# Forgetting attention on one core: second exponentials in place, normalizing one step later, VectorE's work in written order

## The chip, the cores and the metric

The kernel runs on one core of one Trainium2 chip. The metric is the device time of one execution in microseconds, the median of the runs shown; smaller is better. One core has a matrix engine (TensorE, PE in the profile; its weight loads are PEld), a vector engine (VectorE, DVE), a scalar engine (ScalarE, ACT), GpSimd (POOL) and a sync engine (SyncE, SP) that here only issues transfers. Each engine works through its own list of instructions in order, and waits where an instruction's inputs or buffers are not ready. SBUF is the memory that the engines work from, PSUM the one into which TensorE adds up its products; VectorE and ScalarE reach both.

## The reference

The model has two layers over 1024 tokens of width 1024. Layer 0 mixes by causal pooling, layer 1 by forgetting attention; both add a cross-attention into 256 memory tokens, gate the two, project, and end in a layer norm of `ALPHA * x + projection`. The change lies in layer 1's attention:

```python
q = u.reshape(B, S, FOX_HEADS, FOX_HEAD_DIM)          # 16 heads of 64
scale = FOX_HEAD_DIM ** -0.5
def block(args):                                       # one block of 128 queries
    logits = jnp.einsum('bqhd,bkhd->bhqk', qi, k) * scale
    logits = logits + (ci[..., :, None] - cum_k[:, :, None, :])
    mask = kpos[None, :] <= qpos[:, None]
    logits = jnp.where(mask[None, None], logits, -jnp.inf)
    p = jax.nn.softmax(logits, axis=-1)
    return jnp.einsum('bhqk,bkhd->bqhd', p, v)
```

`cum` is the running sum of the log forget gates, one row for each head. Since softmax is unchanged by a constant for each query, the kernel drops `ci` and takes only the row `cum_k` off. Inputs and result are float32.

## The kernel before

To hold the precision of float32, every operand of a product is split in two: a high half in 16 bits and a low half with what the high one leaves out. A product is then two or three products of halves, added up in PSUM.

Around the attention lie the pooling layer and the memory attention before it, and the output projection with the last layer norm after it. The attention itself (`fox`, 16 heads, in pairs `pr` of 0 to 7) takes about 400 of the 1191 us in heads 2 to 15 alone. A head has eight steps, one for each tile of 128 queries, from tile 7 (all 1024 keys) down to tile 0 (128 keys). One step, for tile t:

- `probs`: TensorE makes the logits in parts of up to 512 keys (line 323), each in one of three PSUM banks with the name L. Tile 7 has parts of 512 and 512, tile 6 512 and 384, tile 5 512 and 256, tile 4 384 and 256; tiles 3 to 0 have one part. VectorE reads a part (line 1028, one custom instruction), adds the forget row R, or for the last part the row with the mask in it (`raw`, written by GpSimd at line 1002 three steps ahead), keeps the extreme of each query, and writes to a tile p in SBUF (name MK, four buffers). ScalarE then takes the exponentials (line 1036) into PSUM (name T, two banks) and adds them up into `sums`.
- `inverse_of`: VectorE makes 1/sum from one or two sums (lines 1046, 1048, 1049).
- `halves`: ScalarE multiplies a part by 1/sum and rounds it to the high half (line 1064), VectorE multiplies again and takes the high half off (line 1065), which leaves the low half. Both go into a pair, a tile of halves with the name P, four buffers. In the code these two functions are called for the tile before: the inverse behind this tile's first logits, the halves behind its last.
- `turn`: a transfer on SyncE's queue transposes the pair (line 1081) into one of six buffers T. Tiles 3 and 2, and tiles 1 and 0, share a pair, so a head has six transposes.
- `values`: TensorE multiplies transposed halves by the values (line 1090), six steps later, in one PSUM bank O: tiles 4 to 7 in the second step of the next head, tiles 0 to 3 in its sixth. ScalarE and VectorE combine the bank's halves (lines 1107, 1108). For odd heads GpSimd multiplies by the gate (line 1117) and the result is stored (line 1119).

Between these, `fill.pump` lets TensorE run pieces of other projections (line 359: keys, queries, values and gates of later heads), so many columns per step that they last until the pair of heads ends. Their weights come in 512 KB transfers on SyncE's queue (line 332) into ten buffers with the name B; GpSimd splits them into halves (lines 176, 178, 193) in buffers w. Their results (bank pj) are read by ScalarE and VectorE (lines 912 and 913, 816 and 817, 375 and 376). During heads 14 and 15 the halves of the output projection's weights are split too (lines 198 on ScalarE, 199 on VectorE, and GpSimd).

The order on TensorE is the order in which the code is written (`tc.manual_schedule(engines={PE})`). On the other engines a scheduler sets the order by a cost model of its own, but for the instructions that `tc.keep_in_program_order` pins to their written order; before the change these are GpSimd's masks and gate products and some of the splits. Buffers of a name are handed out in turn, and a new owner waits until the last reader of the old one is done.

## Time and profile before

Three runs took 1191.08, 1191.49 and 1192.35 us.

| what | value |
|---|---|
| time, median of three runs | 1191.49 us |
| profiled execution, its own time | 1193.08 us |
| its span | 1191.4 us |
| TensorE's granted clock | 0.995 |
| TensorE busy, whole span | 1166.9 us (98%) |
| VectorE busy | 782.7 us (66%) |
| ScalarE busy | 684.8 us (57%) |
| GpSimd busy | 286.0 us (24%) |

A row of the trace has the start in us from the span's start, the duration in us, engine, line, operation, output and inputs, the shape, and how many instructions were put together (x2); in brackets stands the idle time ahead of it and who ended that. Numbers behind a line's instructions with slashes are the least, the median and the most of the durations in nanoseconds. In a list of waits a row has the engine, what it was to write, its line, the engine, name and line that released it, and then the sum in us, the number of times and the longest.

### The profile page before, as it was taken

The numbers are of one execution on the slowest core, as the hardware profiler recorded it, in microseconds if no ns is written. First come the engines' busy times: TensorE is split into PE (matmuls) and PEld (weight loads), VectorE is DVE, ScalarE is ACT, GpSimd is POOL, SyncE is SP. The second block draws the span as 40 slices with busy tenths as digits, with TensorE's granted clock in tenths as the row PEclk, the third lists the DMA queues.
The fourth block names the chain that finished last, engine by engine and source line by source line (L and its number), as shares of the span: only waits on it lengthen the run. The fifth ranks groups of instructions, "written<-read, shape, count | busy, mean of one in ns | idle before, by whom it ended". The sixth has DMA issues, their size and how long they took to land. (4 is left out here: it accounts for less than half of the span.)

```text
span 1191.4 us, 19838 instructions
## 1 busy us (share of the span) xinstructions
PE 1166.9 (98%) x6941; PEld 672.7 (56%) x6941; DVE 782.7 (66%) x1840; ACT 684.8 (57%) x1512; POOL 286.0 (24%) x437
## 2 busy tenths in 40 slices
PE   8999999999999999999999999999999999999996
PEld 5566766555555557556664555555555545455553
DVE  5754675555765557357645888778877788884654
ACT  6578875875663234467421776666766677674210
POOL 3322001310000000000002454555555444760000
PEclk9999999999999999999999999999999999999999
DMA  7576656854385555445734789989996899965430
GB/s 261 176 247 198 165 103 208 255 173 148 101 283 160 152 137 134 110 142 108 197 124 113 172 181 221 187 174 204 191 211 147 168 197 205 238 166 169 175 108 35
DMA packets 286196, 203.88 MB, mean 171 GB/s; under 512 B 224913, under 2 KB 238353, under 8 KB 286097
## 3 DMA queue, kind: packets, MB, share of 16 engines
q1 hardware_dynamic: 279696, 181.59, 61.2%
q0 software_dynamic: 6400, 21.04, 5.5%
q8 instruction: 54, 0.88, 0.3%
q14 instruction: 46, 0.37, 0.1%
HBM read 116.01 MB, written 22.61 MB: 116 GB/s over the span
## 5 line engine op out<-in xcount | busy, mean ns | idle before, releaser
L359 PE MATMUL pj<-A,w 128*128 128x512 f16 (+2 forms) x2896 | 662.9, 383 | 1.9 <-ACT MK L200 0.6
L359 PEld LDWEIGHTS <-w 128*128 128x128 f16 (+1 forms) x2560 | 245.6, 98 | 278.3 <-issue 9.5
L1036 ACT ACTIVATE T<-MK,s 128x512 f32<-128x512 f32 x192 | 111.2, 579 | 65.9 <-DVE s L1028 48.8
L1065 DVE SCALAR_TENSOR_TENSOR P<-T,s,P 128x512 f16<-128x512 f32 x192 | 112.0, 613 | 39.1 <-ACT P L1064 37.9
L1064 ACT ACTIVATE P<-T,s 128x512 f16<-128x512 f32 x192 | 102.9, 576 | 53.3 <-issue 28.9
L599 PEld LDWEIGHTS <-T 128*128 128x128 bf16 x736 | 70.6, 98 | 89.2 <-issue 4.4
L1002 POOL TENSOR_SCALAR_AFFINE_SELECT raw<-R 128x256 f32<-128x256 f32 (+3 forms) x128 | 59.8, 468 | 185.5 <-DVE s L1028 102.0
L323 PE MATMUL L<-A 128*128 128x512 f16 (+3 forms) x384 | 84.8, 326 | 5.5 <-DVE s L1028 5.4
L199 DVE TENSOR_TENSOR w<-raw,w 128x512 bf16<-128x512 f32 x74 | 52.0, 703 | 53.9 <-ACT w L198 37.9
L885 POOL MEMSET G<- 128x128 f32 x1 | 0.2, 204 | 334.9 <-DVE V L541 334.9
L359 PEld LDWEIGHTS pj<-A,w 128*128 128x128 f32 x352 | 65.2, 188 | 17.0 <-ACT w L198 1.3
L199 DVE TENSOR_TENSOR T<-T,T 128x1024 bf16<-128x1024 f32 x23 | 28.1, 1220 | 70.2 <-PE pj L599 38.2
L323 PEld LDWEIGHTS <-A 128*128 128x128 f16 x384 | 37.3, 98 | 48.9 <-issue 7.6
L178 POOL TENSOR_TENSOR w<-B,w 128x512 f16<-128x512 f32 x54 | 63.2, 1172 | 4.0
L198 ACT CAST T<-T 128x1024 fp32r<-128x1024 f32 x23 | 24.1, 1047 | 64.0 <-DMA T<-y1d 34.4
L198 ACT CAST w<-raw 128x512 fp32r<-128x512 f32 x76 | 46.8, 615 | 23.9 <-DMA raw<-in_win_dram 10.6
L1090 PEld LDWEIGHTS <-V 128*64 128x64 f16 (+1 forms) x1152 | 50.6, 104 | 13.0 <-issue 5.6
L1090 PE MATMUL O<-T,V 128*64 128x128 f16 (+1 forms) x1152 | 57.5, 221 | 0.1
L599 PE MATMUL pj<-B,T 128*128 128x512 bf16 (+1 forms) x192 | 53.1, 385 | 0.0
L1028 DVE CUSTOM_DVE_ANT_0 MK<-L,R,scales 128x512 f32<-128x512 f32 x64 | 45.3, 708 | 9.7 <-PE L L323 9.4
L200 ACT CAST w<-raw 128x512 bf16<-128x512 f32 x78 | 48.2, 618 | 3.3 <-PE pj L359 1.9
L599 PE MATMUL L<-B,T 128*128 128x512 bf16 (+1 forms) x168 | 47.3, 394 | 0.0
(289 smaller groups left out, 1850.0 us busy)
## 6 DMA issues: line engine op xcount, KB each, us to landing
raw<-in_win_dram SPq DMA_DIRECT2D x66, 256.0 KB, 3.4
W<-in_win_dram POOLq DMA_DIRECT2D x48, 256.0 KB, 4.2
R<-cumd SPq DMA_DIRECT2D x16, 512.0 KB, 4.6
B<-in_win_dram SPq DMA_DIRECT2D x15, 512.0 KB, 4.9
y0d<-Y SPq DMA_DIRECT2D x12, 512.0 KB, 4.0
raw<-in_wout_dram SPq DMA_DIRECT2D x24, 256.0 KB, 2.7
T<-y0d SPq DMA_DIRECT2D x12, 512.0 KB, 4.2
A<-A SPq DMA_DIRECT2D x24, 256.0 KB, 4.0
```

The costliest lines, as they stand in the source:

```text
L178: pin(nc.gpsimd.tensor_tensor(to.lo, src, to.hi, ALU.subtract))
L198: pin(nc.scalar.copy(to.hi, src))
L199: pin(nc.vector.tensor_tensor(to.lo, src, to.hi.bitcast(F32), ALU.subtract))
L200: pin((top or nc.scalar.copy)(to.top, src))
L323: nc.tensor.matmul(acc, a, b, start=i == 0, stop=i == len(terms) - 1)
L359: nc.tensor.matmul(accs[n], a[:, k, :], b[:, pc * 4 + k, n * NH : (n + 1) * NH], start=seen[n] == 1, stop=seen[n] == 3 * KT,)
L599: nc.tensor.matmul(accs[a][nh], y, w, start=kt == 8 and i == 0, stop=kt == 7 and i == 2,)
L1002: tc.keep_in_program_order(nc.gpsimd.affine_select(C[:, :w], R[:, lo:up], [[-1, w]], ALU.is_ge, -NEG, base=w - P, channel_multiplier=1,))
L1036: nc.scalar.activation(e, p[:, lo:up], AF.Exp, bias=top, scale=-1.0, accum_out=sums[:, n, hd % 2, i : i + 1],)
L1064: nc.scalar.activation(pair[:, lo:up], e, AF.Copy, scale=r)
L1065: nc.vector.scalar_tensor_tensor(pair[:, L + lo : L + up], e, r, pair[:, lo:up], ALU.mult, ALU.subtract)
L1090: nc.tensor.matmul(acc[rows, (i % 4) * P : (i % 4) * P + P], v[:, b, 2 * j : 2 * j + (1 if e else 2), :].rearrange("p e d -> p (e d)"), pt ...
```

## The change

The change is confined to `fox` and the functions that it calls. The line numbers in the changed file are a little other ones: logits 1025, exponentials 1032, inverse 1043, 1045 and 1046, high halves 1061, low halves 1066, transposes 1085, combining of the values 1111 and 1112.

- Where a tile has two parts, the exponential of the second is written in place, over the logits in the tile p in SBUF, and no longer into a PSUM bank T. The two halves of that part are then made from SBUF. This holds for all heads.
- VectorE's logits, inverses and low halves are pinned to the order in which they are written. `halves` is taken apart into `high_halves` (ScalarE) and `low_half` (VectorE).
- In heads 0 to 13, the inverse and the high halves of a tile are written behind the exponentials of the next tile, and its low halves behind the logits of the tile after that: one low half behind the first logits, the rest behind the last.
- In heads 14 and 15, low halves that are left over and the inverse are written behind the first logits, high and low halves of the tile before behind the last.
- In heads 0 to 13 the pair of tile 7, that of tile 5 and the one that tiles 1 and 0 share are buffers with the name B. The pairs of tile 6, of tile 4 and of tiles 3 and 2 stay buffers P.

```diff
-        def probs(hd, i, R, sums, inverse, behind):
+        def probs(hd, i, R, sums, behind):
...
-                nc.vector.tensor_tensor_reduce(p[:, lo:up], lg, rows, unq, top, ALU.add, ALU.min, m[:, n : n + 1])
+                tc.keep_in_program_order(
+                    nc.vector.tensor_tensor_reduce(p[:, lo:up], lg, rows, unq, top, ALU.add, ALU.min, m[:, n : n + 1])
+                )
                 top = m[:, n : n + 1]
-                if n == 0:
-                    inverse()
-            behind()
+                behind(n, n == len(parts) - 1)
             es = []
             for n, (lo, up) in enumerate(parts):
-                e = ps([P, NH], "T", 2)[:, : up - lo]
+                e = p[:, lo:up] if n else ps([P, NH], "T", 2)[:, : up - lo]
...
-        def halves(hd, i, es, r):
+        def high_halves(hd, i, es, r):
...
-                pair = sb([P, 2 * S], "P", 4, F16)
+                pair = xy([P, 2 * S], F16) if hd < HEADS - 2 and i in (7, 5, 1) else sb([P, 2 * S], "P", 4, F16)
...
             for lo, up, e in es:
                 nc.scalar.activation(pair[:, lo:up], e, AF.Copy, scale=r)
-                nc.vector.scalar_tensor_tensor(pair[:, L + lo : L + up], e, r, pair[:, lo:up], ALU.mult, ALU.subtract)
-            return hd, i, pair
+            return pair
+
+        def low_half(i, r, pair, lo, up, e):
+            L = (i + 1) * P
+            tc.keep_in_program_order(nc.vector.scalar_tensor_tensor(
+                pair[:, L + lo : L + up], e, r, pair[:, lo:up], ALU.mult, ALU.subtract,
+            ))
...
+                    def highs():
                         if fresh[0]:
-                            split.append(halves(*fresh[0]))
+                            old, k, es, r = fresh[0]
+                            pair = high_halves(*fresh[0])
+                            waiting.append((old, k, [(k, r, pair, *e) for e in es], pair))
                             fresh[0] = None
+
+                    def lows(every):
+                        while waiting:
+                            old, k, left, pair = waiting[0]
+                            low_half(*left.pop(0))
+                            if not left:
+                                split.append((old, k, pair))
+                                waiting.pop(0)
+                            if not every:
+                                break
+
+                    def behind(n, last):
+                        if pr < 7:
+                            lows(last)
+                            return
+                        if n == 0:
+                            lows(True)
+                            inverse()
+                        if last:
+                            highs()
+                            lows(True)
...
-                        fresh[0] = probs(hd, tile_of, R, sums, inverse, behind)
+                        made = probs(hd, tile_of, R, sums, behind)
+                        if pr < 7:
+                            inverse()
+                            highs()
+                        fresh[0] = made
                     else:
                         inverse()
-                        behind()
+                        highs()
+                        lows(True)
```

TensorE's 12270 instructions stand in the same order before and after, and no engine computes more or less. What moves, at three places:

VectorE in head 3, from tile 6's first logits to tile 5's (MK is p, L a logits bank, s small columns such as 1/sum, P or B the pair, O the values' bank, G the head's result; each logits instruction is followed by one that reads out its extreme), before:

```order
L1028 ISA MK_7434,s_7435<-L_7436,R_7054,scales 128x512
L1028 ISA s_7435 128x1
L1046 TENSOR_SCALAR s_7440<-sums_7014 128x1
L1028 ISA MK_7434,s_7435<-L_7443,raw_7323,s_7435,scales 128x384
L1028 ISA s_7435 128x1
L1049 RECIPROCAL s_7440<-s_7440 128x1
L1065 SCALAR_TENSOR_TENSOR P_7447<-T_7406,s_7440,P_7447 128x512
L1065 SCALAR_TENSOR_TENSOR P_7447<-T_7408,s_7440,P_7447 128x512
L1108 SCALAR_TENSOR_TENSOR G_7013<-O_7458,scales,G_7013 64x512
L1028 ISA MK_7520,s_7521<-L_7522,R_7054,scales 128x512
```

And the same place after:

```order
L1025 ISA MK_7418,s_7419<-L_7420,R_7042,scales 128x512
L1025 ISA s_7419 128x1
L1066 SCALAR_TENSOR_TENSOR B_7354<-T_7349,s_7392,B_7354 128x128
L1025 ISA MK_7418,s_7419<-L_7425,raw_7310,s_7419,scales 128x384
L1025 ISA s_7419 128x1
L1043 TENSOR_SCALAR s_7432<-sums_7005 128x1
L1046 RECIPROCAL s_7432<-s_7432 128x1
L1112 SCALAR_TENSOR_TENSOR G_7004<-O_7440,scales,G_7004 64x512
L1025 ISA MK_7502,s_7503<-L_7504,R_7042,scales 128x512
L1025 ISA s_7503 128x1
L1066 SCALAR_TENSOR_TENSOR B_7435<-T_7389,s_7432,B_7435 128x512
L1025 ISA MK_7502,s_7503<-L_7509,raw_7338,s_7503,scales 128x256
```

Tile 7's two low halves moved from ahead of the combining of the values and tile 5's logits to behind tile 5's first logits (the second of them stands two rows below the piece), and tile 0's low half, of the head before, stands among tile 6's logits.

ScalarE at the same place, from tile 7's second exponential on, before:

```order
L1036 ACTIVATE T_7408,sums_7014<-MK_7391,s_7392 128x512
L1064 ACTIVATE P_7447<-T_7406,s_7440 128x512
L1064 ACTIVATE P_7447<-T_7408,s_7440 128x512
L1107 ACTIVATE G_7013<-O_7458,scales 64x512
L1036 ACTIVATE T_7452,sums_7014<-MK_7434,s_7435 128x512
L1036 ACTIVATE T_7454,sums_7014<-MK_7434,s_7435 128x384
```

And after:

```order
L1032 ACTIVATE MK_7378,sums_7005<-MK_7378,s_7379 128x512
L1061 ACTIVATE B_7354<-T_7349,s_7392 128x128
L1032 ACTIVATE T_7429,sums_7005<-MK_7418,s_7419 128x512
L1032 ACTIVATE MK_7418,sums_7005<-MK_7418,s_7419 128x384
L1061 ACTIVATE B_7435<-T_7389,s_7432 128x512
L1061 ACTIVATE B_7435<-MK_7378,s_7432 128x512
L1111 ACTIVATE G_7004<-O_7440,scales 64x512
L912 ACTIVATE A_3341<-pj_7396 128x512
```

Tile 6's exponentials moved ahead of tile 7's high halves and of the combining of the values. Heads 1, 4 to 6, 8 to 10 and 12 have this order too; in heads 2, 7, 11 and 13 the combining stands ahead of tile 6's exponentials.

SyncE's queue, which takes transfers in order: before, part of the stretch ahead of the attention (lines 509 and 835 belong to the memory attention and the first values, 332 to the weights of later heads):

```order
L332 DMA B_6561<-in_win_dram 128x2x512
L509 DMA_TRANSPOSE T_5584<-P_5547 128x16x128
L332 DMA B_6781<-in_wk_dram 128x2x512
L332 DMA B_7038<-in_win_dram 128x2x512
L332 DMA B_7317<-in_wv_dram 128x2x512
L509 DMA_TRANSPOSE T_5663<-P_5626 128x16x128
```

After, the first transposes of the attention, with the first two of the same loads:

```order
L1085 DMA_TRANSPOSE T_6471<-B_6423 128x16x128
L1009 DMA R_6688<-cumd 128x1024
L1085 DMA_TRANSPOSE T_6513<-P_6462 128x14x128
L1085 DMA_TRANSPOSE T_6545<-B_6502 128x12x128
L332 DMA B_6553<-in_win_dram 128x2x512
L1085 DMA_TRANSPOSE T_6581<-P_6538 128x10x128
L1085 DMA_TRANSPOSE T_6644<-P_6575 128x14x128
L1085 DMA_TRANSPOSE T_6714<-B_6635 128x6x128
L332 DMA B_6771<-in_wk_dram 128x2x512
```

Nine weight loads moved from ahead of the attention to places among its transposes, since buffers B are now handed out in turn to loads and pairs.

More of the change, by code (lines that the diff above doesn't have):

```diff
@@ L1044, in inverse_of @@
             one, two = (sums[:, n, hd % 2, i : i + 1] for n in range(2))
+            pin = tc.keep_in_program_order
             if n == 2:
-                nc.vector.tensor_scalar(r, one, two, 1.0 / PSCALE, ALU.add, ALU.mult)
+                pin(nc.vector.tensor_scalar(r, one, two, 1.0 / PSCALE, ALU.add, ALU.mult))
             else:
-                nc.vector.tensor_scalar(r, one, 1.0 / PSCALE, None, ALU.mult)
-            nc.vector.reciprocal(r, r)
-            return r
-        joined = []
-        def halves(hd, i, es, r):
+                pin(nc.vector.tensor_scalar(r, one, 1.0 / PSCALE, None, ALU.mult))
+            pin(nc.vector.reciprocal(r, r))
+            return r
+        shared = []
+        def high_halves(hd, i, es, r):
             L = (i + 1) * P
             if i in (2, 0):
-                pair = joined.pop()[:, 2 * L + 2 * P :]
+                pair = shared.pop()[:, 2 * L + 2 * P :]
             else:
-                pair = sb([P, 2 * S], "P", 4, F16)
+                pair = xy([P, 2 * S], F16) if hd < HEADS - 2 and i in (7, 5, 1) else sb([P, 2 * S], "P", 4, F16)
                 if i in (3, 1):
-                    joined.append(pair)
+                    shared.append(pair)
             for lo, up, e in es:
                 nc.scalar.activation(pair[:, lo:up], e, AF.Copy, scale=r)
-                nc.vector.scalar_tensor_tensor(pair[:, L + lo : L + up], e, r, pair[:, lo:up], ALU.mult, ALU.subtract)
-            return hd, i, pair
+            return pair
[4 more added lines that the diff above has]
+            ))
+        joined = []
         pt = {}
@@ L1133, in fox @@
         def fox(following, out_proj, head):
-            fill, past, fresh = Fill(), [None] * LAG, [None]
+            fill, past, fresh, waiting = Fill(), [None] * LAG, [None], []
             def two_lines(row):
```

1 line of the change is left out of this document (removed).

## The prediction

> **What bounds the kernel now.** I read the busy shares first, then a table of the engines over the stretch of the forgetting attention after its first two heads (heads 2 to 15), then what TensorE waits for there, then those waits one by one.
>
> ```profile
> span 1191.4 us, 19838 instructions
> PE 1166.9 (98%) x6941; PEld 672.7 (56%) x6941; DVE 782.7 (66%) x1840; ACT 684.8 (57%) x1512; POOL 286.0 (24%) x437
> sum 401.00, PE 395.46 PEld 207.78 DVE 318.30 ACT 279.81 POOL 210.09; mean PE 43.94 PEld 23.09 DVE 35.37 ACT 31.09 POOL 23.34
> PE L L323 <- DVE s L1028: 5.4, 8, 2.1
> 702.35 0.38 PE L323 MATMUL L<-A 128*128 128x256 f16 x2 [0.24 <-DVE s L1028]
> 725.73 0.38 PE L323 MATMUL L<-A 128*128 128x256 f16 x2 [0.53 <-DVE s L1028]
> 828.33 0.38 PE L323 MATMUL L<-A 128*128 128x256 f16 x2 [0.43 <-DVE s L1028]
> 930.93 0.38 PE L323 MATMUL L<-A 128*128 128x256 f16 x2 [0.45 <-DVE s L1028]
> 971.09 0.48 PE L323 MATMUL L<-A 128*128 128x384 f16 x2 [0.26 <-DVE s L1028]
> 978.44 0.38 PE L323 MATMUL L<-A 128*128 128x256 f16 x2 [1.11 <-DVE s L1028]
> 1024.49 0.48 PE L323 MATMUL L<-A 128*128 128x384 f16 x2 [0.32 <-DVE s L1028]
> 1034.07 0.38 PE L323 MATMUL L<-A 128*128 128x256 f16 x2 [2.05 <-DVE s L1028]
> ```
>
> TensorE is busy for 395.46 of 401.00 us of that stretch. Nearly all that is missing are eight waits, listed one by one, for VectorE to read a logits bank: 0.24 + 0.53 + 0.43 + 0.45 + 0.26 + 1.11 + 0.32 + 2.05 = 5.39 us. The order of TensorE's instructions is the same before and after, so these 5.39 us are all that the change can win, and the floor is 1191.49 - 5.39 = 1186.1 us. The profiled execution took 1193.08 us (span 1191.4), 1.59 above the median of the three runs; I take the sum as a difference and set it against the median. VectorE (318.3 us) and ScalarE (279.8) have room in the stretch: their order matters, not their sums.
>
> **Why TensorE waits.** Logits go through three banks in turn, so the second part of tile 4 needs the bank of the first part of tile 5, called L5.0 below (L6.1 is the second part of tile 6, lo7 and hi7 are tile 7's halves, O1 the combining of the values' result). Head 3, from TensorE, ScalarE and VectorE:
>
> ```profile
> 719.38 2.48 PE L1090 MATMUL O<-T,V 128*64 128x128 f16 x52
> 724.72 0.49 PE L323 MATMUL L<-A 128*128 128x384 f16 x2
> 722.24 1.26 ACT L1064 ACTIVATE P<-T,s 128x512 f16<-128x512 f32 x2 [1.03 <-issue]
> 723.53 0.69 ACT L1107 ACTIVATE G<-O,scales 64x512 f32<-64x512 f32 x1
> 717.17 0.48 DVE L1065 SCALAR_TENSOR_TENSOR P<-T,s,P 128x256 f16<-128x256 f32 x1
> 722.95 1.41 DVE L1065 SCALAR_TENSOR_TENSOR P<-T,s,P 128x512 f16<-128x512 f32 x2 [0.80 <-ACT P L1064]
> 724.28 0.73 DVE L1108 SCALAR_TENSOR_TENSOR G<-O,scales,G 64x512 f32<-64x512 f32 x1
> 724.94 0.73 DVE L1028 CUSTOM_DVE_ANT_0 MK<-L,R,scales 128x512 f32<-128x512 f32 x1
> DVE P L1065 <- ACT P L1064: 37.9, 61, 0.8
> ACT T L1036 <- DVE P L1065: 16.6, 42, 0.8
> ```
>
> TensorE is through with tile 4's first part at 724.72 + 0.49 = 725.21, and L5.0 ends at 724.94 + 0.73 = 725.67. On VectorE it stands behind lo7 (which waited 0.80 for ScalarE's hi7) and behind O1, which follows ScalarE's part of O1, itself behind hi7. The sums of such waits are the last two rows.
>
> **The change, step by step.** It adds and removes no computing instruction; what it does is order, buffers and two waits.
>
> First, the second exponential goes into SBUF, so tile t+1's exponentials no longer wait for a second PSUM bank that the low halves give back. That removes some of the 16.6 us of ScalarE waits, worth nothing by itself: ScalarE has 121 us of room.
>
> Second, L5.0 now stands ahead of lo7. In heads 2, 7, 11 and 13 ScalarE's order becomes exponentials 7, hi of tile 0, O1, exponentials 6. O1 then starts when the values end; in head 3's times that is 719.38 + 2.48 = 721.86, ScalarE's part to 722.55, VectorE's to 723.3, L5.0 to 724.0, which is 1.2 before the 725.21 at which it is wanted. The waits of these heads go: 0.24 + 0.43 + 0.45 + 0.26 + 1.11 = 2.49 us won.
>
> Third, in heads 1, 3 to 6, 8 to 10 and 12 the order becomes exponentials 6, hi7, O1. In head 3 the chain starts at most 0.6 earlier than now, since the 0.48 us low half at 717.17 no longer precedes the logits. Exponentials 7 then end near 720.6, 6 near 721.95, hi7 (1.26) 723.2, O1 on ScalarE 723.9, on VectorE 724.65, L5.0 725.4; without the earlier start 726.0. The wait of 0.53 becomes 0.2 to 0.8; I take 0.5, no gain. Heads 6, 10 and 12 lose what they had, as L5.0 stood ahead of O1 there:
>
> ```profile
> 804.71 0.71 PE L323 MATMUL L<-A 128*128 128x384 f16 x4
> 799.87 0.68 DVE L1028 CUSTOM_DVE_ANT_0 MK<-L,raw,s 128x384 f32<-128x384 f32 x1
> 802.76 0.74 DVE L1028 CUSTOM_DVE_ANT_0 MK<-L,R,scales 128x512 f32<-128x512 f32 x1
> 803.77 0.76 DVE L1108 SCALAR_TENSOR_TENSOR G<-O,scales,G 64x512 f32<-64x512 f32 x1 [0.26 <-ACT G L1107]
> ```
>
> Head 6 had 1.7 us of room (803.50 against some 805.2). With the change tile 6's logits end at 799.87 + 0.68 = 800.55 as before, exponentials 6 at 802.0, hi7 at 803.2, O1 at 803.9 and 804.65, L5.0 at 805.4: a wait of 0.2 to 0.4, 0.3 by my choice, in three heads 0.9 us lost. Head 1 is like head 3: 0.4 lost. Heads 4, 5, 8 and 9 have longer steps: none.
>
> Fourth, heads 14 and 15 keep the old order but for the lows of the tile before, which go behind the first logits.
>
> ```profile
> 1023.69 0.73 DVE L1028 CUSTOM_DVE_ANT_0 MK<-L,R,scales 128x512 f32<-128x512 f32 x1
> 1027.35 0.21 DVE L1046 TENSOR_SCALAR s<-sums 128x1 f32<-128x1 f32 x1 [1.59 <-ACT T L1036]
> 1031.39 0.21 DVE L1046 TENSOR_SCALAR s<-sums 128x1 f32<-128x1 f32 x1 [0.82 <-ACT T L1036]
> 1033.28 0.73 DVE L1028 CUSTOM_DVE_ANT_0 MK<-L,R,scales 128x512 f32<-128x512 f32 x1
> ```
>
> Head 15's first logits, at 1023.69 behind a product of the gate, start some 2 us sooner, which frees the 0.32. L5.0, at 1033.28, is wanted near 1034.07 - 2.05 = 1032.0 and should be read by 1030.4 if the whole head moves up by those 2 us and the inverse no longer waits for a PSUM bank; if not, only the 0.32 is won. I take both, 2.37, since the waits of 1.59 and 0.82 in front are of the kind that the change loosens.
>
> Fifth, highs and lows come later, the transposes of the pairs with them. In heads 3, 6, 10 and 12 tile 4's goes out 1 to 2 us later. Closest is head 6's:
>
> ```profile
> 814.40 3.14 SPq L1081 DMA_TRANSPOSE T<-P  x1
> 822.07 2.48 PE L1090 MATMUL O<-T,V 128*64 128x128 f16 x52
> DMA to landing us min/median/max: 2.8/4.7/7.5
> ```
>
> It lands about 1.2 us before the product. Between nothing and 1.5 us a head in four heads: 0 to 6 us. I take 0.5, as two steps lie between in most heads.
>
> Sixth, tile 7, 5 and 1's pairs sit in the buffers of the weights, which are handed out in written order, so nine 512 KB weight loads that now are issued before the attention begins stand among the attention's transposes.
>
> ```profile
> DMA to landing us min/median/max: 3.8/4.9/9.4
> 754.43 2.80 SPq L1081 DMA_TRANSPOSE T<-P  x1
> 767.84 3.19 PE L359 MATMUL pj<-A,w 128*128 128x512 f16 x14
> L178 POOL TENSOR_TENSOR w<-B,w x54: 1153/1157/1656, 625.0 to 1040.4; 128x512 f16<-128x512 f32 x54
> ```
>
> The closest is the value weight in head 4: the transpose ahead of it ends at 757.2, the load lands 4.9 later at 762.1, GpSimd takes about 3.9 (three steps of that size and their waits) to the first pieces, 766.0; TensorE asks at 767.84. At the median it costs nothing, with 1.8 to spare; at 9.4 it is 2.7 late. I take 0.5.
>
> Sum: -2.49 - 2.37 + 0.9 + 0.4 + 0.5 + 0.5 = -2.56: 1191.49 - 2.56 = 1188.9. Its own range is 1186.5 (no new waits but the small ones) to 1190.6 (head 15 keeps most of its wait).
>
> **Rivals.** A: nothing moves that a run can tell (within 0.2% either way). For it: heads 6, 10 and 12 may wait the 0.5 of head 3, and head 15 may keep its 2.05. The sum is then -2.49 - 0.32 + 1.5 + 0.4 + 1.0 = 0.1 us: 1191.6.
>
> B, slower: the weight loads land late. They now queue behind transposes of 2 to 3 us. If they take the 9.4 us and not 4.9, head 4's is 2.7 late and the two next in tightness some 1.5 each (my estimate: a microsecond more of room), with nothing else for TensorE to run: 5.7 + 0.5 for the transposes against the 3.56 that the second to fourth steps win, +2.6: 1194.1. It decides from a landing of 6.7 us (4.9 + 1.8) on. Against it: the median is 4.9 and the slow ones fell among other wide loads.
>
> C, slower: the transposes are late by the 1.5 us of the fifth step in all four heads, 6 + 0.5 against 3.56, +2.9: 1194.4. Against it: tile 4's low halves stood two steps back before, too.
>
> D, slower: the low halves of the second parts now read both inputs from SBUF (the exponential was in PSUM), and a like subtraction with both inputs there is slower while GpSimd works:
>
> ```profile
> L1065 DVE SCALAR_TENSOR_TENSOR P<-T,s,P x192: 339/610/752, 655.4 to 1053.3; 128x512 f16<-128x512 f32 x80, 128x384 f16<-128x384 f32 x48, 128x256 f16<-128x256 f32 x48, 128x128 f16<-128x128 f32 x16
> L199 DVE TENSOR_TENSOR w<-raw,w x52: 679/692/695, 102.0 to 499.6; 128x512 bf16<-128x512 f32 x52
> L199 DVE TENSOR_TENSOR B<-B,B x4: 681/948/1643, 1010.1 to 1048.1; 128x512 bf16<-128x512 f32 x4
> ```
>
> Sixty-four instructions (four tiles of 16 heads) by 0.948 - 0.692 = 0.26 us are 17 us on VectorE, about 1 us a head. Most of it stands behind L5.0 and in VectorE's 83 us of room; a third of it on the path is 5.7, against the 2.56 of the forecast +3.1: 1194.6; it decides from about 15% on the path. [...]
>
> **Chances.** The forecast 0.47, A 0.28, B 0.09, C 0.08, D 0.08. What a measurement of this kernel can tell is about 0.2%, or 2.4 us. Faster by more (below 1189.1): 0.34, two thirds of the forecast and a little of A; within it: 0.41, the rest of both; slower (above 1193.9): 0.25, being B, C and D. The range is 1186.3, the floor with a little left over, to 1195.0, which takes in A and the lower half of B to D, whose prices could double.
>
> **What would show it.** Right: the waits of TensorE for logits near 2 us in place of 5.4, gone in heads 2, 7, 11, 13 and at the end of head 15, small ones in 3, 6, 10, 12; L5.0 ahead of lo7. Wrong: TensorE waiting for GpSimd's pieces of weights (B), for a transpose (C), low halves from SBUF longer than their fellows from PSUM (D), or head 15's wait still at 2 us (A).

## The result and the profile after

The changed kernel takes 1211.99 us (median of five runs, 1209.77 to 1213.91), the kernel before 1191.08 (1190.09 to 1192.35). The ratio is 1.0172, with a 95% interval of 1.0161 to 1.0184: 20.9 us slower, where 2.6 us faster was forecast. The profiled execution of the changed kernel took 1210.2 us, that of before 1193.08, so the two traces show 17.1 of the 20.9 us. TensorE begins the first logits of head 0 at 645.05 us of the span after and at 649.26 before, and the first product behind the attention (line 599) at 1067.67 and 1050.28. So the attention takes 422.6 us in place of 401.0, a loss of 21.6 us, and 4.2 us were won ahead of it, where a wait of TensorE of 2.1 us at line 848 is gone, and with it the stretch behind that wait, 602.99 to 606.40 us of the span before, in which the granted clock was 0.50.

The page of the changed kernel (span and busy times), and behind it its waits: TensorE's, and the two of VectorE and ScalarE in the attention that grew most:

```profile
span 1208.5 us, 19766 instructions
PE 1170.7 (97%) x6894; PEld 673.3 (56%) x6941; DVE 784.2 (65%) x1840; ACT 685.9 (57%) x1512; POOL 300.7 (25%) x437
```

```profile
PE L L323 <- DVE s L1025: 11.9, 12, 2.4
PE pj L359 <- POOL w L193: 5.4, 3, 3.2
PE O L1094 <- DMA T<-P: 2.7, 3, 1.2
PE pj L359 <- POOL w L178: 0.3, 1, 0.3
...
DVE G L1112 <- ACT G L1111: 36.2, 16, 3.1
ACT T L1032 <- DVE P L1066: 27.1, 39, 1.4
```

Before, TensorE waited 5.4 us for logits to be read, and in the attention not at all for weights from GpSimd or for transposes. Now it waits 11.9, 5.7 and 2.7. VectorE waited 2.5 us for ScalarE's part of the combining of the values, as a row of before shows, now 36.2:

```profile
DVE G L1108 <- ACT G L1107: 2.5, 9, 0.3
```

ScalarE's exponentials wait 27.1 us for low halves where they waited 16.6, although the second of them no longer needs a bank of PSUM.

A part of the loss is in no wait. Three of TensorE's waits are followed by a stretch at a lower granted clock. The table by stretch of time has the length, TensorE's busy time with its instructions, the granted clock, the transfers' share and GB/s; the three stretches stand right behind the waits (in brackets) of the three rows of the timeline after it:

```profile
726.00:730.60 4.60, 4.50 (x15) 0.63 0.71 194
773.80:778.40 4.60, 4.54 (x14) 0.63 1.10 236
969.40:973.40 4.00, 3.94 (x12) 0.57 0.24 46
```

```profile
726.10 0.38 PE L323 MATMUL L<-A 128*128 128x256 f16 x2 [2.31 <-DVE s L1025]
773.86 4.88 PE L359 MATMUL pj<-A,w 128*128 128x512 f16 x14 [3.19 <-POOL w L193]
969.46 0.58 PE L323 MATMUL L<-A 128*128 128x256 f16 x2 [2.37 <-DVE s L1025]
```

4.6 x 0.37, 4.6 x 0.37 and 4.0 x 0.43 are 1.7 us each, 5.1 us together, an estimate from the length of the stretches and their clock. The sum in the attention is 11.9 + 5.7 + 2.7 + 5.1 = 25.4 us in place of 5.4: 20.0 of the 21.6 us are accounted for.

Head 3 has two of the longer waits. Rows of the changed kernel, of TensorE, ScalarE and VectorE:

```profile
712.07 1.03 PE L323 MATMUL L<-A 128*128 128x512 f16 x4
717.16 0.48 PE L323 MATMUL L<-A 128*128 128x384 f16 x2 [1.27 <-DVE s L1025]
723.31 0.49 PE L323 MATMUL L<-A 128*128 128x384 f16 x2
...
719.70 0.35 ACT L1061 ACTIVATE B<-T,s 128x128 f16<-128x128 f32 x1
721.30 0.69 ACT L1032 ACTIVATE T<-MK,s 128x512 f32<-128x512 f32 x1 [1.26 <-DVE s L1025]
723.92 0.69 ACT L1111 ACTIVATE G<-O,scales 64x512 f32<-64x512 f32 x1
...
715.75 0.69 DVE L913 SCALAR_TENSOR_TENSOR A<-pj,A 128x512 f16<-128x512 f32 x1 [1.16 <-ACT A L912]
716.36 0.74 DVE L1025 CUSTOM_DVE_ANT_0 MK<-L,R,scales 128x512 f32<-128x512 f32 x1
720.08 0.35 DVE L1066 SCALAR_TENSOR_TENSOR B<-T,s,B 128x128 f16<-128x128 f32 x1 [0.92 <-ACT B L1061]
720.58 0.68 DVE L1025 CUSTOM_DVE_ANT_0 MK<-L,raw,s 128x384 f32<-128x384 f32 x1 [0.15 <-PE O L1094]
724.64 0.74 DVE L1112 SCALAR_TENSOR_TENSOR G<-O,scales,G 64x512 f32<-64x512 f32 x1 [3.05 <-ACT G L1111]
725.31 0.73 DVE L1025 CUSTOM_DVE_ANT_0 MK<-L,R,scales 128x512 f32<-128x512 f32 x1
```

Tile 7's logits are made from 712.07 to 713.1, and VectorE first reads them at 716.36, since a result of another projection stands ahead, for which ScalarE is late. Then the two engines wait for each other in turn. VectorE's reading of tile 6's second logits (720.58) stands behind the low half of tile 0, which waits for ScalarE's high half (719.70), which stands behind tile 7's exponentials. ScalarE waits for that reading with tile 6's exponentials (721.30), then come tile 7's high halves, then the combining (723.92). VectorE waits 3.05 us for the combining, and tile 5's logits, behind it, end at 726.04. TensorE had wanted the bank at 723.31 + 0.49 = 723.8 and waits 2.31.

### The profile page after: what moved, and what is told of

It is laid out like the page before. It is cut to its first block, busy times and chain, and to the rows that moved or that the text cites. A ratio compares the mean times of both kernels' runs of the same rounds, so it can differ in the third digit from the quotient of the medians.

```text
span 1208.5 us, 19766 instructions
## 1 busy us (share of the span) xinstructions
PE 1170.7 (97%) x6894; PEld 673.3 (56%) x6941; DVE 784.2 (65%) x1840; ACT 685.9 (57%) x1512; POOL 300.7 (25%) x437
## 4 chain that ended last, share of the span: by engine, by line
PE 71%; DVE 11%; ACT 7%; issue 5%; DMA 4%; POOL 2%; SPq 0%; DVEq 0%; ACTq 0%; POOLq 0%
PE pj L359 37%; PE L L599 9%; PE pj L599 9%; PE L L323 3%; DVE MK L1025 3%; PE O L1094 3%; PE pj L410 2%; PE L L492 2%; DVE P L1066 2%; PE pj L848 2%; ACT B L1061 1%; DMA T<-P 1%; PE T L599 1%; ACT T L1032 1%; DVE B L1066 1%
## 5 line engine op out<-in xcount | busy, mean ns | idle before, releaser
L1032 ACT ACTIVATE T<-MK,s 128x512 f32<-128x512 f32 (+3 forms) x128 | 76.4, 597 | 101.8 <-DVE s L1025 72.5
L1002 POOL TENSOR_SCALAR_AFFINE_SELECT raw<-R 128x256 f32<-128x256 f32 (+3 forms) x128 | 69.1, 545 | 147.8 <-DVE s L1025 99.8
L323 PE MATMUL L<-A 128*128 128x512 f16 (+3 forms) x384 | 85.6, 327 | 11.9 <-DVE s L1025 11.9
L359 PEld LDWEIGHTS pj<-A,w 128*128 128x128 f32 x352 | 65.1, 188 | 16.6 <-ACT w L198 1.5
L1066 DVE SCALAR_TENSOR_TENSOR P<-T,s,P 128x512 f16<-128x512 f32 (+1 forms) x72 | 48.3, 671 | 19.0 <-ACT P L1061 18.5
L198 ACT CAST w<-raw 128x512 fp32r<-128x512 f32 x76 | 46.8, 615 | 24.0 <-DMA raw<-in_win_dram 10.7
L1061 ACT ACTIVATE P<-T,s 128x512 f16<-128x512 f32 (+1 forms) x72 | 44.5, 619 | 20.7 <-issue 6.0
L176 POOL TENSOR_SCALAR B<-B,scales 128x512 f32<-128x512 f32 x54 | 39.8, 738 | 53.9 <-DMA B<-in_win_dram 25.9
```

Of the source, the lines that this page charges most:

```text
L198: pin(nc.scalar.copy(to.hi, src))
L323: nc.tensor.matmul(acc, a, b, start=i == 0, stop=i == len(terms) - 1)
L359: nc.tensor.matmul(accs[n], a[:, k, :], b[:, pc * 4 + k, n * NH : (n + 1) * NH], start=seen[n] == 1, stop=seen[n] == 3 * KT,)
L1002: tc.keep_in_program_order(nc.gpsimd.affine_select(C[:, :w], R[:, lo:up], [[-1, w]], ALU.is_ge, -NEG, base=w - P, channel_multiplier=1,))
L1032: nc.scalar.activation(e, p[:, lo:up], AF.Exp, bias=top, scale=-1.0, accum_out=sums[:, n, hd % 2, i : i + 1],)
L1061: nc.scalar.activation(pair[:, lo:up], e, AF.Copy, scale=r)
```

## The experiments

The kernel before ran beside each group of kernels on the same chip; its medians were 1191.74 us beside those named e, 1191.62 beside f and 1190.68 beside g. The waits in the table are TensorE's in the attention, in us, from each kernel's profiled execution; a fall is a stretch behind a wait in which the granted clock was 0.50. The last column is VectorE's wait for ScalarE's part of the combining.

| kernel | us | ratio to before (95%) | logits | weights | transposes | falls | combining |
|---|---|---|---|---|---|---|---|
| before | 1191.08 | | 5.4 | 0 | 0 | 0 | 2.5 |
| changed | 1211.99 | 1.0172 (1.0161, 1.0184) | 11.9 | 5.7 | 2.7 | 3 | 36.2 |
| e1_in_place_only | 1196.01 | 1.0032 (1.0022, 1.0042) | 7.0 | 0 | 0.4 | 0 | 2.2 |
| e2_old_steps | 1196.89 | 1.0046 (1.0028, 1.0064) | 11.3 | 1.8 | 0 | 0 | 16.1 |
| e3_no_pins | 1194.11 | 1.0016 (1.0004, 1.0027) | 1.3 | 3.4 | 2.7 | 1 | 1.5 |
| e4_pairs_in_P | 1209.46 | 1.014 (1.011, 1.017) | 14.8 | 0.6 | 0.2 | 4 | 38.3 |
| f1_no_pins_pairs_in_P | 1191.19 | 0.9988 (0.9975, 1.0001) | 3.8 | 0 | 0.8 | 0 | 1.9 |
| f2_combine_behind | 1216.84 | 1.0200 (1.0183, 1.0218) | 3.5 | 9.9 | 11.3 | 3 | 16.0 |
| f3_one_copy | 1197.70, one run | | 11.2 | 0 | 0 | 1 | 5.0 |
| f4_two_copies | 1206.68, one run | | 16.5 | 0.6 | 0.2 | 1 | 4.2 |
| g1_pins_on_before | 1199.77 | 1.0065 (1.0050, 1.0081) | 12.9 | 0 | 0 | 0 | 17.3 |
| g2_lows_free | 1211.41 | 1.0176 (1.0150, 1.0201) | 17.8 | 2.0 | 1.4 | 2 | 1.6 |
| g3_inverse_free | 1201.27 | 1.0082 (1.0060, 1.0105) | 5.0 | 5.6 | 0.3 | 1 | 22.9 |
| g4_late_all_free | 1192.21 | 1.0010 (1.0001, 1.0020) | 3.0 | 0 | 1.3 | 0 | 3.1 |

### One part alone, and one part undone

The second exponential in place, in the kernel before:

```diff
-                e = ps([P, NH], "T", 2)[:, : up - lo]
+                e = p[:, lo:up] if n else ps([P, NH], "T", 2)[:, : up - lo]
```

> The kernel before with one line changed: the second part's exponential goes into p in SBUF. Theory (the order and the weights cost the 21 us, not the place of the exponential): within 2 us of the kernel before, 1189 to 1193 us, no load waits by GpSimd that were not there. Rival (low halves that read both inputs from SBUF are slower, D of the prediction): at least half of the 21 us, over 1200 us, and the low halves of second parts longer than 0.75 us.

It is 4.3 us slower, between the two. Rows by shape of the low halves, first from PSUM (T), then from SBUF (MK), in this kernel (count, busy us, mean ns):

```profile
L1065 DVE SCALAR_TENSOR_TENSOR P<-T,s,P 128x512 f16<-128x512 f32 x64 | 48.0, 750 | 31.0 <-ACT P L1064 30.1
L1065 DVE SCALAR_TENSOR_TENSOR P<-MK,s,P 128x512 f16<-128x512 f32 x16 | 15.4, 963 | 0.0
L1065 DVE SCALAR_TENSOR_TENSOR P<-MK,s,P 128x256 f16<-128x256 f32 x32 | 18.6, 582 | 0.0
L1065 DVE SCALAR_TENSOR_TENSOR P<-T,s,P 128x256 f16<-128x256 f32 x15 | 7.2, 482 | 1.5 <-ACT P L1064 1.5
```

From SBUF they do take longer: 16 x 0.21 + 32 x 0.10 and, for 384 keys (0.696 against 0.615 us), 16 x 0.08, together 7.9 us on VectorE. Of the 16 with 512 elements, six had no GpSimd instruction beside them and took 0.74 us, ten had one and took 1.09 on the average. TensorE's waits grow by 1.6 us for logits and 0.8 us for a transpose and a projection's result. That is 2.4 of the 4.3 us; what the rest is, this run does not show. Nor does it show that the longer low halves make the waits: the scheduler gave VectorE another order too (in head 3 the combining stands behind tile 5's first logits, before it stood ahead of them). ScalarE's wait for low halves fell from 16.6 to 3.8 us.

The steps of before, with all else of the change kept:

```diff
-                        if pr < 7:
-                            lows(last)
-                            return
                         if n == 0:
...
-                        if pr < 7:
-                            inverse()
-                            highs()
```

> The changed kernel with 1/sum and halves back in the steps of before in all heads; in place, pinned order and pairs in the weights' buffers stay. Theory (the later step makes the logits waits): the waits of TensorE for logits fall from 11.9 to 6 us or less and the time by 6 to 11 us, to 1201 to 1206 us; the waits for weights of 5.7 us stay. Rival (the pinned order makes them): no change, 1210 to 1214 us.

15.1 us are won, more than expected, but not where the theory had it: the waits for logits stay at 11.3. What goes are the waits over 1.7 us with their falls of the clock, two thirds of those for weights, and those for transposes. So the later step does not make the logits waits, it makes them long in some places.

The pinned order taken away, with all else kept:

```diff
-                tc.keep_in_program_order(
-                    nc.vector.tensor_tensor_reduce(p[:, lo:up], lg, rows, unq, top, ALU.add, ALU.min, m[:, n : n + 1])
-                )
+                nc.vector.tensor_tensor_reduce(p[:, lo:up], lg, rows, unq, top, ALU.add, ALU.min, m[:, n : n + 1])
...
-            pin = tc.keep_in_program_order
+            pin = lambda ins: ins
...
-            tc.keep_in_program_order(nc.vector.scalar_tensor_tensor(
+            nc.vector.scalar_tensor_tensor(
                 pair[:, L + lo : L + up], e, r, pair[:, lo:up], ALU.mult, ALU.subtract,
-            ))
+            )
```

> The changed kernel without the pinned order on VectorE; in place, later step and pairs in the weights' buffers stay. Theory (later step): the waits for logits stay near 12 us and the time within 4 us of 1212. Rival (the pinned order makes them): they fall below 6 us and the time to 1201 to 1206 us.

The rival holds, and by more than it said: 17.9 us are won. Head 3 of this kernel on VectorE and TensorE:

```profile
721.63 0.75 DVE L1064 SCALAR_TENSOR_TENSOR B<-T,s,B 128x512 f16<-128x512 f32 x1 [0.16 <-ACT B L1059]
722.30 0.74 DVE L1024 CUSTOM_DVE_ANT_0 MK<-L,R,scales 128x512 f32<-128x512 f32 x1
722.97 0.74 DVE L1110 SCALAR_TENSOR_TENSOR G<-O,scales,G 64x512 f32<-64x512 f32 x1
722.77 0.71 PE L323 MATMUL L<-A 128*128 128x384 f16 x4
```

Tile 5's logits stand ahead of the combining and are read at 722.30, TensorE makes both parts of tile 4's logits in one go, and no wait is left. The head's steps are the late ones.

All pairs in P again, with the pinned order and the later step:

```diff
-                pair = xy([P, 2 * S], F16) if hd < HEADS - 2 and i in (7, 5, 1) else sb([P, 2 * S], "P", 4, F16)
+                pair = sb([P, 2 * S], "P", 4, F16)
```

> The changed kernel with all pairs in the four buffers P again; everything else stays. Theory (weights wait since their buffers are handed out in turn with pairs): the nine loads go ahead of the attention again, TensorE's 5.7 us of waits for weights vanish with one of the three falls of the clock, 1203 to 1206 us. Rival (four buffers are too few for pairs that are kept longer): new waits of ScalarE for pairs, and 1212 us or more.

The waits for weights do go, 5.7 to 0.6, but the waits for logits grow to 14.8, another of 2.2 us ahead of the values' products comes, which ends with ScalarE, and there are four falls. The median is 2.5 us lower, which four runs from 1204.40 to 1211.71 us do not tell from nothing. Neither side holds: ScalarE does not wait for pairs, and the time is above the theory's.

Both together, free order and pairs in P:

> The changed kernel without the pinned order and with all pairs in P; in place and the later step stay. Theory (pinned order makes the logits waits, pairs among the weights' buffers the waits for weights; the later step itself is good): TensorE waits for logits at most 1.5 us and for weights under 1 us, no fall of the clock, 1187 to 1190 us, faster than before. Rival (four P are too few for the later step): waits for pairs or transposes, 1193 us or more.

1191.19 us, against 1191.62 of the kernel before on the same chip: no difference that the runs can tell, 2.9 us better than with the pairs among the weights' buffers. The waits for weights and the fall of the clock are gone; the waits for logits are 3.8 us where at most 1.5 were expected, and the 1187 to 1190 us were not reached. In head 15, which has the old steps, a wait of 2.22 us stays. The later step there too:

```diff
                     def behind(n, last):
-                        if pr < 7:
+                        if pr < 8:
                             lows(last)
                             return
...
-                        if pr < 7:
+                        if pr < 8:
                             inverse()
                             highs()
```

> As the kernel without pinned order and with all pairs in P, and the later step in heads 14 and 15 too. Theory (the later step takes the logits waits away where VectorE's order is free): head 15's wait of 2.2 us goes below 0.5, the waits for logits are 1.7 us or less in all, 1188 to 1190 us, faster than before. Rival (four P run out beside the output projection's splits): new waits in heads 14 and 15, 1192 us or more.

The wait in head 15 falls to 1.54 us only, where less than 0.5 was expected, and 1.4 us of waits for the gates' results come beside it. With 1192.21 us the kernel is 1.5 us slower than the one before on the same chip: the theory missed, and no version here beats the kernel before.

### Is it the combining, or the queue?

The combining of the values written and pinned behind the next tile's first logits:

```diff
-            nc.scalar.activation(oc, acc[other, :], AF.Copy, scale=un[own])
-            nc.vector.scalar_tensor_tensor(oc, acc[own, :], un[own], oc, ALU.mult, ALU.add)
+            def combine():
+                nc.scalar.activation(oc, acc[other, :], AF.Copy, scale=un[own])
+                tc.keep_in_program_order(nc.vector.scalar_tensor_tensor(oc, acc[own, :], un[own], oc, ALU.mult, ALU.add))
+
+            return combine
...
                     def behind(n, last):
+                        if n == 0:
+                            while later:
+                                later.pop(0)()
```

> The changed kernel with the combining of the values (ScalarE's and VectorE's part) written, and on VectorE pinned, behind the next tile's first logits; all else stays. Theory (in pinned order the combining holds up tile 5's logits, 36 us of VectorE waits): the waits for logits fall from 11.9 to 3 us or less, two of the three falls of the clock go, about 9 + 3.4 us are won, 1198 to 1202 us; the 5.7 us for weights and one fall stay. Rival (VectorE is late from earlier in the head, the combining only passes it on): the waits for logits stay over 8 us, 1207 us or more.

In the lines left out, the gate's product and the store of odd heads move behind the combining too. The waits for logits fall near to the 3 us of the theory, to 3.5, but the time rises by 4.8 us. Rows of this kernel's waits:

```profile
PE O L1094 <- DMA T<-P: 11.3, 5, 3.6
PE pj L359 <- POOL w L193: 9.9, 5, 5.8
PE L L323 <- DVE s L1025: 3.5, 5, 1.5
...
DVE MK L1025 <- PE L L323: 38.6, 23, 6.5
```

VectorE now stands 38.6 us before logits that TensorE has not made yet (13.4 in the changed kernel), and TensorE waits 11.3 us for transposes and 9.9 for weights. Why these are late, this run does not isolate: low halves stand behind those logits in the pinned order, but the gate's product and the store moved as well. What it does show is that another place for the combining trades waits for logits against other waits, and does not win the time back.

### Which pins

The pins alone, in the kernel before:

```diff
-                nc.vector.tensor_tensor_reduce(p[:, lo:up], lg, rows, unq, top, ALU.add, ALU.min, m[:, n : n + 1])
+                tc.keep_in_program_order(
+                    nc.vector.tensor_tensor_reduce(p[:, lo:up], lg, rows, unq, top, ALU.add, ALU.min, m[:, n : n + 1])
+                )
...
-                nc.vector.scalar_tensor_tensor(pair[:, L + lo : L + up], e, r, pair[:, lo:up], ALU.mult, ALU.subtract)
+                tc.keep_in_program_order(
+                    nc.vector.scalar_tensor_tensor(pair[:, L + lo : L + up], e, r, pair[:, lo:up], ALU.mult, ALU.subtract)
+                )
```

and the same around the three instructions of `inverse_of`.

> The kernel before with VectorE's logits, inverses and low halves pinned to their written order, and nothing else. Theory (the pinned order makes the logits waits by itself): waits of TensorE for logits of 9 to 14 us in place of 5.4, none for weights or transposes, 1194 to 1200 us. Rival (only the pinned order with the later step makes them): 5 to 6.5 us of waits and 1190 to 1193 us.

9.1 us slower, and the trace has 7.5 of it as waits for logits:

```profile
PE L L323 <- DVE s L1029: 12.9, 11, 1.6
...
DVE G L1113 <- ACT G L1112: 17.3, 16, 1.5
```

Eleven waits, none over 1.6 us and no fall of the clock. So the pinned order makes the waits by itself. With the later step they become longer than 2 us in places.

The changed kernel with one kind of instruction freed:

```diff
-            tc.keep_in_program_order(nc.vector.scalar_tensor_tensor(
+            nc.vector.scalar_tensor_tensor(
                 pair[:, L + lo : L + up], e, r, pair[:, lo:up], ALU.mult, ALU.subtract,
-            ))
+            )
```

> The changed kernel with the low halves not pinned; logits and inverses stay pinned. Theory (a low half that waits for ScalarE's high half holds up the logits behind it): waits for logits fall from 11.9 to under 6 us, 1199 to 1205 us. Rival (the inverses, which wait for exponentials, hold them up): waits near 12 us, 1208 us or more.

```diff
-            pin = tc.keep_in_program_order
+            pin = lambda ins: ins
```

> The changed kernel with the inverses not pinned; logits and low halves stay pinned. Theory (low halves): waits for logits near 12 us, 1208 us or more. Rival (inverses): under 6 us and 1199 to 1205 us.

Freed low halves win nothing, freed inverses 10.7 us: in both kernels the numbers are the rival's, which blames the inverses. The first does not clear the low halves: freed, they went back ahead of tile 5's logits in the list of VectorE's instructions, where they wait for the high halves, and the waits for logits rose to 17.8 us while that for the combining fell to 1.6. The second removes more than half of the waits for logits (5.0). Between the pinned inverses and the pinned low halves a wait moves about; only without any pins do both sums become small. Pinned logits alone were not run.

### The clock

One or two copies ahead of the reading of tile 5's first logits, in every head of the kernel before:

```diff
+                for _ in range(1 if i == 5 and n == 0 else 0):
+                    nc.vector.tensor_copy(p[:, lo:up], lg)
                 nc.vector.tensor_tensor_reduce(p[:, lo:up], lg, rows, unq, top, ALU.add, ALU.min, m[:, n : n + 1])
```

> The kernel before with one more VectorE instruction in each head: a copy of tile 5's first logits, about 0.6 us, ahead of their own reading. Theory (a wait of TensorE of over some 2.2 us lowers the granted clock for some 4 us, which costs about 1.7 us beside the wait): the waits of before at tile 4 grow by about 0.6 each; the one of head 15 (2.05) passes 2.2 and a fall of the clock follows it, the others (0.9 to 1.7) have none. Rival (the clock falls from the sum of waits in a longer time, not from one): falls after shorter waits as well, or none at 2.65.

> As the kernel with one copy, with two copies: tile 4's waits about 1.2 us longer than before. Theory: falls of the clock only after waits over 2.2 us, heads 13 (1.11 + 1.2) and 15 (2.05 + 1.2), each 7 or 8 matmuls of 0.43 us; heads 2, 3, 7, 11 (1.4 to 1.8) have none. Rival: falls after waits of 1.4 to 1.8 us too, or none.

With one copy, six waits between 1.0 and 1.3 us, three of 0.2 and one of 3.31; only the last is followed by a fall, twelve products 0.43 us apart. With two copies the one of 3.35 us has a fall behind it and the one of 2.33 has none. That is not the theory's 2.2 us. The waits in the attention of all the kernels sort like this:

| wait, us | followed by a fall | not followed |
|---|---|---|
| below 2.0 | 1.78, in the kernel with all pairs in P | all others |
| 2.0 to 2.4 | 2.00, 2.01, 2.05, 2.17, 2.31, 2.37, 2.37 | 2.05, 2.07, 2.11, 2.17, 2.19, 2.22, 2.33, 2.36 |
| 3.1 to 3.3 | 3.19 | 3.22 |
| over 3.3 | 3.31, 3.35, 3.35, 3.38, 3.44, 3.64, 5.83 | none |

Two rows of the kernel with free low halves show that length alone does not tell them apart, the first behind a wait of 3.22 us, the second behind one of 2.01:

```profile
703.70:708.00 4.30, 4.24 (x21) 1.00 0.60 112
994.50:999.00 4.50, 4.41 (x15) 0.64 1.03 292
```

The traces' records of the granted clock say when the falls begin: in the changed kernel at 727.09, 774.88 and 969.43 us, which are 14 and 57 steps of 3.413 us apart. Each of the 16 in the attention lasts one such step, 3.41 us, or two. Below, a trace is cut into windows of one step, counted forward and back from its falls. The table by stretch of time has four of these windows of the kernel with free low halves (TensorE's busy time stands behind the length, the granted clock behind the brackets):

```profile
698.83:702.24 3.41, 1.71 (x9) 1.00 0.25 48
702.24:705.66 3.42, 1.90 (x10) 1.00 0.74 139
992.37:995.79 3.42, 1.41 (x9) 1.00 1.08 168
995.79:999.20 3.41, 3.41 (x10) 0.50 1.15 326
```

The wait of 3.22 us lies across the border of two windows, with 1.70 and 1.52 us idle in them, and the clock stays at 1.00. That of 2.01 us lies whole in one window, and in the next one the clock is 0.50. In the changed kernel TensorE was idle for 2.31, 2.40 and 2.34 us in the windows ahead of the three falls; behind one with 1.81 the clock was 1.00. Counted like this in all fourteen traces, from 20 to 1180 us of the span, the clock fell behind all 16 windows in which TensorE was idle for 2.0 us or more, behind one of the three with 1.78, 1.81 and 1.97, and behind none with 1.70 or less. So in these traces what told the waits of 2 to 3.3 us apart was how much of them lay in one window. Why it is so is not shown, nor how the waits lie in a kernel's other executions, since each kernel has one trace.

## Why the prediction was wrong

**What bounds.** Right as far as it goes: the loss is TensorE's waits and what follows from them, since the order of its work did not move.

**The first step**, that in-place exponentials free ScalarE from waiting for low halves and cost nothing, is half right. Alone, the edit takes that wait from 16.6 to 3.8 us; in the changed kernel it is 28.8 (1.7 of it for pairs among the weights' buffers), since the first parts still take a bank of T each and the low half that gives it back stands later, pinned behind logits (9.4 us with the steps of before, 8.3 without the pins). But the term for it was nothing, and alone the edit costs 4.3 us. Rival D foresaw longer low halves, with 17 us on VectorE; measured are 7.9, and how much of the 4.3 they make is not shown. Of the four slower subtractions that it rested on (line 199, from 1010.1 us of the span before), two took 0.68 us, one with a GpSimd instruction beside it and one without, and two with one took 1.21 and 1.64.

**The second step** was right where it looked: the waits in heads 7, 11 and 13 went, 2.25 us of the 2.49. Head 2 now waits 0.63 instead of 0.24.

**The third step** is the one that failed. It walked through a head from the same start as before, "at most 0.6 earlier", and put small waits of 0.3 to 0.5 us into heads 1, 3, 6, 10 and 12. Its walk, from the first reading of tile 7's logits to the end of tile 5's, comes out for head 6: 9.7 us forecast (from 795.70 to 805.4), 9.57 measured, and the same in heads 8, 10 and 12. In head 3 it is 9.68 us where 8.4 was forecast; there tile 0's low half, pinned ahead of tile 6's second logits, waits 0.92 us for ScalarE. And heads start later against TensorE: head 3 reads its first logits 4.3 us after TensorE began them (712.07 and 716.36), before 2.3 (715.29 and 717.58); head 6 1.5 us after, before 0.6; head 12 3.2, before 2.1. The lateness comes from the end of the head before, where the two engines wait for each other in turn. At the end of head 2 ScalarE's exponentials wait 1.24 and 0.68 us for low halves, VectorE 0.56 for a high half and 1.16 for a projection's result that ScalarE makes behind them. For head 12 the step also took head 6's room of 1.7 us; the trace of before shows 0.4 there (tile 5's logits end at 953.62, wanted at 954.05). Waits of heads 1, 3, 6, 10 and 12 came to 0.81, 3.58, 1.03, 1.21 and 2.58 us, sum 9.2 in place of the predicted 1.8; heads 8 and 14 (0.80, 1.11) and head 4 (0.18) had none in the prediction. The prediction held that VectorE and ScalarE, with 83 and 121 us of room, would absorb such waits. Here, where two queues wait for each other in a fixed order, the room did not absorb them; e3_no_pins, the same steps in free order, has 1.3 us of waits for logits.

**The fourth step** was right: both waits of head 15 went, 2.37 us. 0.32 us behind a weight's pieces came in their place. It was close: tile 5's logits end at 1050.90 and are wanted at 1051.33.

**The fifth step** took 0.5 us for late transposes; measured are 2.7, less than half of rival C's 6, and in heads 3, 7 and 11, where heads 3, 6, 10 and 12 were named.

**The sixth step** took 0.5 us for the weights; measured are 5.7, and 1.7 more for the fall behind the longest. Rival B was right on the effect, and its 5.7 us by luck, since its condition was wrong: transfers did not land later (median 4.8 us, at most 7.3, against 4.9 and 9.4). They were issued later. A row of SyncE's waits, and the timeline of its queue and of GpSimd around the load in question:

```profile
SPq L1009 <- POOL raw L1002: 22.5, 10, 5.3
```

```profile
755.42 1.32 SPq L1085 DMA_TRANSPOSE T<-B  x1
762.11 0.34 SPq L1009 DMA_DIRECT2D R<-cumd  x1
764.58 1.04 SPq L332 DMA_DIRECT2D B<-in_wv_dram  x1
754.05 0.69 POOL L176 TENSOR_SCALAR B<-B,scales 128x512 f32<-128x512 f32 x1 [5.26 <-DMA B<-in_win_dram]
761.61 1.04 POOL L1002 TENSOR_SCALAR_AFFINE_SELECT raw<-R 128x128 f32<-128x128 f32 x2
770.12 0.69 POOL L176 TENSOR_SCALAR B<-B,scales 128x512 f32<-128x512 f32 x1 [6.30 <-DMA B<-in_wv_dram]
```

Ahead of the value weight stands the next head's forget row, and it goes out only when a mask that GpSimd makes at 761.61 is done. GpSimd worked without a pause from 754.05, when a wait of 5.26 us for another weight's load ended, and the mask stood behind that weight's pieces and a gate's product: one late load held up the next. SyncE's queue stood there for 5.3 us; the load went out at 764.58, and TensorE waited 3.19 us behind it. The step had counted the time from the end of the transpose ahead, not what that queue waits for.

**Not in the prediction at all**: the falls of the clock, 5.1 us. The trace of before has one such fall too, ahead of the attention, at 602.99 us behind the wait of 2.1 us at line 848.

**The sum** was -2.56 us; by its own terms it is +20.0 in the trace: 6.5 for logits (against -3.6), 2.7 for transposes (0.5), 5.7 for weights (0.5) and 5.1 for the clock (0). By the runs, the pins make the larger part: without them the change costs 2.4 us, alone they cost 9.1, and together 20.9. Of the 2.4, e3's trace shows 3.4 for weights with one fall, and f1, with the pairs back in P, is level with before. What the two parts cost together beyond their sum is the waits above 2 us with their falls, and the late transposes and loads.

## What to carry to other kernels

To read a build's list of instructions gives the order of a queue but not when its head stands still: before an engine's order is fixed by hand, follow for each instruction that waits for another engine which instructions behind it that engine in turn waits for, from the head before on and not from a clean start. A transfer that moves into a shared queue is late by whatever the queue's head waits for, a buffer's release among it, so count that and not the landing time: here SyncE's queue stood 5.3 us for a mask, a weight's load behind it. Behind a long wait of TensorE, read the granted clock in the trace as well: here three waits of 2.31, 3.19 and 2.37 us, 7.9 in all, had 3.41 us at a clock of 0.50 behind each, 5.1 us more by the estimate above.

## What was not expected of the hardware

The granted clock fell to 0.50 behind all 16 windows of 3.413 us, counted from a trace's falls, in which TensorE had been idle for 2.0 us or more, in fourteen traces; behind one of the three with 1.78, 1.81 and 1.97, and behind none with 1.70 or less. A wait of 3.22 us that lay across two windows, with 1.70 and 1.52 in them, had no fall; one of 2.01 us in a single window had one. A fall lasted 3.41 us and cost 1.7 by the estimate from its length and clock; three lasted 6.83 us, of which 0.8 to 1.3 were still wait, and cost some 2.8 to 3.0 by an estimate from half the rest.

A subtraction on VectorE that reads both inputs from SBUF took 0.74 us for 512 elements with no GpSimd instruction beside it, and 1.09 on the average and up to 1.62 with one (six and ten instructions of the kernel with only the exponentials in place). With one input in PSUM, in the kernel before, it took 0.748 on the average and at most 0.752, both in the 31 instructions with no GpSimd instruction beside them and in the 49 with one.
